# Retention projections of a two-layer hybrid trunk: blocks of 256 weight columns become blocks of 512, with six weight slots and tokens in pairs

## Chip, core and metric

One core of a Trainium2 chip runs the whole kernel. The metric is the device time of one execution in microseconds (us), as the median of three runs. The profile is of one more execution.

## What is computed

Two layers work on a residual stream of 1024 tokens by 1024 features. In each, one projection makes everything that the token mixer needs: queries, keys, values and forget logits of eight attention heads (64 wide), and queries, keys, values and gates of four retention heads (128 wide). The retention part, cut to what matters here:

```
rq, rk, rv, rg = x @ w_in[:, ...]            # (1024 tokens) x (4 heads x 128) each
q = rotary(rq); k = rotary(rk) * 128**-0.5
for each chunk of 128 tokens:
    o = (q k^T * decay) v + (q * xi) state
    state = chunk_decay * state + (k * zeta)^T v
out = silu(rg) * groupnorm(o) * gain
```

After it come the attention heads, one output projection with a layer norm, and a feed-forward part (1024 to 4096 to 1024, squared ReLU) with a second layer norm. All of it is float32; the matrix products are split (below).

## The kernel before

**Products.** Each float32 operand is split into a high part, rounded to the matrix engine's reduced float32 type, and a low part, the rest. `split` (L158, L159) makes them: ScalarE (ACT) casts the high part, VectorE (DVE) subtracts for the low one. `mm3` (L220) then makes three matmuls for each slice of 128 input features: low by high, high by low, high by high. In the retention projections the stationary operand is a tile of 128 tokens (`act`), and the moving operand is the weights (`whi`, `wlo`).

**Weights.** `load_next` takes the next key of one fixed order, starts a DMA on SyncE's queue into one of two staging buffers (`wst`, L205), and splits it into one of four slots (`whi`, `wlo`, a ring of `RING = 4`). `weight(key)` asks for a key and calls `load_next` until the two keys after it (`AHEAD = 2`) are emitted. A key is always 512 KB: here 512 input features by 256 columns, so that a block of 256 columns has two keys.

**The stage.** `retention(l, r, ...)` runs twice in a layer, each time for two of the four heads (256 columns). In each it projects four names one after the other: `rq`, `rk`, `rg`, `rv`. `project(name)` walks over four pairs of token tiles. A pair shares one PSUM bank: two token tiles by 256 columns, 2 x 8 x 3 = 48 matmuls. `bank()` hands out four banks in turn. After a pair, the program first emits what uses the bank, then calls `tick()`, which counts down deferred work, and after every second pair it emits `weight_sums` (L972 to L980): a 1 MB load `wr` from the feed-forward weights, four DVE sums `ts`, and a 1 MB store. These sums are for the feed-forward part.

- `rq` and `rk`: eight DVE instructions rotate a bank (`ra`, `rb`, L393), four GpSimd (POOL) instructions add them up (`nrq`, `nrk`, L398 and L399), and two ticks later four TensorE (PE) transposes (L379) and an ACT copy (L381) follow.
- `rg`: ACT takes the SiLU of a bank (`gt`, L411), POOL multiplies it by the gains (L413).
- `rv`: ACT copies a bank (`rvt`, L463). Two ticks later come the scores and state products (L421, L424), a tick after that the outputs (L441, L443), the group norm, and a store to `r_d` (L455).

After the stage comes the first attention projection (`project_qk`, heads 0 and 1), then attention with the other projections as filling.

**Order.** The program gives the instructions of each engine in this order, but a planner reorders them: the kernel is traced under `tile.TileContext(nc, schedule_with_timeline_sim=True)`, which lays the instructions out by its own estimate of when each could run, the earlier one in the program first among those that are ready. On the chip each engine then goes through its list in that fixed order, and waits on semaphores where an operand or a buffer isn't ready.

**Memory.** Tiles live in pools. Pool `p1v_l` is open for the value projection, `p1r_l` for the stage, `p2_l` for the attention behind it; a later pool takes the memory of an earlier one, and a tile waits for those tiles whose place it takes.

Of the kernel before, what the change touches and what calls it, by code (L numbers as in the profile page):

```python
# [17 lines left out]
P = 128  # L18
# [23 lines left out]
HALF_ROOM = 56  # L42
# [33 lines left out]
def hybrid_trunk(ctx: ExitStack, tc, x, w_in, w_out, w_ff1, w_ff2, ln1_g, ln1_b, ln2_g, ln2_b,  # L76
# [25 lines left out]
    V.memset(half, -0.5)  # L102

# [34 lines left out]
    def defer(n, fn):  # L138
        waiting.append([n, fn])
# [27 lines left out]
    def spec(key, ap):  # L167
        specs[key] = ap
        order.append(key)

    for l in range(L):
# [9 lines left out]
        for r in range(2):  # L181
            for name, c0 in (("rq", C_RQ), ("rk", C_RK), ("rg", C_RG), ("rv", C_RV)):
                block((name, r), c0 + 256 * r, 256)
# [8 lines left out]
    loaded, emitted, odd_home = {}, [0], [None]  # L192

    def load_next(after=None):
        key = order[emitted[0]]
        emitted[0] += 1
        src = specs[key]
        _, kk, cc = src.shape
        odd = key[1] == "vb"
        home, two = (odd_home[0], 1) if odd else (wp, 2)  # L200
        tags = ("vst", f"vhi{key[2]}", f"vlo{key[2]}") if odd else ("wst", "whi", "wlo")
# [123 lines left out]
    def forget_sums(z, pool):  # L325
# [16 lines left out]
        ones = pool.tile([FH, 512], F32, tag="ones", name=nm("ones"), bufs=1)  # L342
        V.memset(ones, 1.0)
# [14 lines left out]
    def retention(l, r, xT, pool, cos, sin, gn, steps):  # L358
        def project(name):
            w = [weight(l, (name, r), g) for g in range(2)]  # L360
            for tp in range(NT // 2):
                ps = bank()
                for j in range(2):
                    mm3(ps[:, 256 * j : 256 * j + 256], lambda a, k: xT.at(a, k, (2 * tp + j) * P, P),
                        lambda b, k: w[k // 4][b][:, k % 4, :], range(8))
                yield tp, ps
                tick()
                steps[0] += 1
                if steps[0] % 2 == 0:
                    weight_sums(l, steps[0] // 2 - 1, ps)  # L370

        def rotate(name, gt, natural):
            trans = []

            def turn(nat):
                tr = ps_tr.tile([P, 2, 2, P], F32, tag="tr", name=nm("tr"))
                for h in range(2):
                    for j in range(2):
                        PE.transpose(tr[:, h, j, :], nat[:, j, h].rearrange("p a d -> p (a d)"), ident)  # L379
                tq = pool.tile([P, 2, 2, P], F32, tag="t" + name, name=nm("t" + name), bufs=4)  # L380
                A.copy(tq, tr)  # L381
                trans.append(tq)

            for tp, ps in project(name):
                p4 = ps.rearrange("p (t h a d) -> p t h a d", t=2, h=2, a=2)
                ra = pool.tile([P, 2, 2, 2, 64], F32, tag="ra", name=nm("ra"), bufs=2)
                rb = pool.tile([P, 2, 2, 2, 64], F32, tag="rb", name=nm("rb"), bufs=2)
                for j in range(2):
                    tt = 2 * tp + j
                    for h in range(2):  # L390
                        sc = gt[:, tt * RH + 2 * r + h : tt * RH + 2 * r + h + 1]
                        for o, tab in ((ra, cos), (rb, sin)):
                            V.scalar_tensor_tensor(o[:, j, h], p4[:, j, h], sc,  # L393
                                                   tab[:, tt, :].unsqueeze(1).broadcast_to([P, 2, 64]),
                                                   op0=ALU.mult, op1=ALU.mult)
                nat = pool.tile([P, 2, 2, 2, 64], F32, tag="n" + name, name=nm("n" + name), bufs=4 if natural is not None else 2)
                for j in range(2):
                    G.tensor_tensor(nat[:, j, :, 0, :], ra[:, j, :, 0, :], rb[:, j, :, 1, :], op=ALU.subtract)  # L398
                    G.tensor_tensor(nat[:, j, :, 1, :], ra[:, j, :, 1, :], rb[:, j, :, 0, :], op=ALU.add)  # L399
                if natural is not None:  # L400
                    natural.append(nat)
                defer(2, lambda nat=nat: turn(nat))
            return trans

        qT = rotate("rq", gq, None)
        kn = []
        kT = rotate("rk", gk, kn)
        gates = []
        for tp, ps in project("rg"):
            gt = pool.tile([P, 2, 256], F32, tag="gt", name=nm("gt"), bufs=4)  # L410
            A.activation(gt.rearrange("p a b -> p (a b)"), ps, AF.Silu)  # L411
            for j in range(2):
                G.tensor_tensor(gt[:, j, :], gt[:, j, :], gn[:, 256 * r : 256 * r + 256], op=ALU.mult)  # L413
            gates.append(gt)
        states = {}

        def scores(tp, j, vt):
            tt = 2 * tp + j
            pa = ps_tr.tile([P, 512], F32, tag="tr", name=nm("tr"))
            for h in range(2):  # L420
                PE.matmul(pa[:, h * P : h * P + P], kT[tp][:, h, j, :], qT[tp][:, h, j, :], start=True, stop=True)  # L421
            if tt < NT - 1:
                for h in range(2):
                    PE.matmul(pa[:, 256 + h * P : 256 + h * P + P], kn[tp][:, j, h].rearrange("p a d -> p (a d)"),  # L424
                              vt[:, j, h, :], start=True, stop=True)
# [10 lines left out]
        def outputs(tp, j, vt, inner):  # L436
            tt = 2 * tp + j
            po = ps_pv.tile([P, 512], F32, tag="pv", name=nm("pv"))
            for h in range(2):
                hs = slice(h * P, h * P + P)  # L440
                PE.matmul(po[:, hs], inner[:, hs], vt[:, j, h, :], start=True, stop=tt == 0)  # L441
                if tt > 0:
                    PE.matmul(po[:, hs], qT[tp][:, h, j, :], states[tt][:, hs], start=False, stop=True)  # L443
# [10 lines left out]
            G.tensor_tensor(on, on, gates[tp][:, j, :], op=ALU.mult)  # L454
            SP.dma_start(r_d[tt * P : tt * P + P, 256 * r : 256 * r + 256], on)  # L455

        def core(tp, vt):
            inner = [scores(tp, j, vt) for j in range(2)]
            defer(1, lambda: [outputs(tp, j, vt, inner[j]) for j in range(2)])

        for tp, ps in project("rv"):
            vt = pool.tile([P, 2, 2, P], F32, tag="rvt", name=nm("rvt"), bufs=3)
            A.copy(vt.rearrange("p a b c -> p (a b c)"), ps)  # L463
            defer(2, lambda tp=tp, vt=vt: core(tp, vt))
# [183 lines left out]
    def layer(l, xT, nxt):  # L648
        src = x if l == 0 else x_d
        with tc.tile_pool(name=f"p1_{l}", bufs=1, reuse_waits="tile") as pool:  # L650
# [521 lines left out]
```

## Time and profile before

| | |
|---|---|
| median of three runs | 2432.82 us (2430.74 to 2435.23) |
| profiled execution, device time | 2434.84 us |
| profiled execution, span from first to last instruction | 2433.1 us |
| PE busy in the span | 2383.8 us, 13424 matmuls |
| DVE, ACT, POOL busy | 1520.0, 1019.9, 376.1 us |
| mean granted clock of PE | 0.997 of full speed |

The profile counts an engine as busy while at least one of its instructions is in flight. Matmuls overlap each other, so the duration of one is longer than the step from the start of one to the start of the next. PEld is the loading of stationary operands, which overlaps PE. A row of a timeline view merges equal neighbours: start, duration of all together, engine (SPq is SyncE's DMA queue), line, operation, out<-in, shape, how many (x), and in brackets the idle time before with what ended it.

### The profile page before, as it was taken

How to read it: one execution, taken by the hardware profiler on the slowest of the kernel's cores; microseconds unless marked ns; L12 is line 12 of the kernel's file. 1: busy time of each engine (PE TensorE's matmuls, PEld its weight loads, DVE VectorE, ACT ScalarE, POOL GpSimd, SP SyncE). 2: the span in 40 equal slices, each digit the busy share in tenths (PEclk: the TensorE clock that was granted, in tenths of full speed). 3: DMA queues.
4: the chain of work that ended last, by engine and by line, in shares of the span. 5: the costliest groups of instructions: out<-in, count | busy, mean ns of one | idle time of the engine just before them, and what ended most of it. 6: DMA issues, size and time to landing. Idle time of an engine off the chain costs nothing. (4 is left out here: it accounts for less than half of the span.)

```text
span 2433.1 us, 35602 instructions
## 1 busy us (share of the span) xinstructions
PE 2383.8 (98%) x13424; PEld 2065.2 (85%) x13424; DVE 1520.0 (62%) x2720; ACT 1019.9 (42%) x1540; POOL 376.1 (15%) x661
## 2 busy tenths in 40 slices
PE   8999999999999999999999999999999999999997
PEld 8999978787888888888899998877888888888886
DVE  4545547855876667565755554578557766576557
ACT  3212236744644453434321222477364545443331
POOL 0324223610000000000213332345000000000003
PEclk9999999999999999999999999999999999999998
DMA  7455685533354458667545566663324544587664
GB/s 231 158 209 202 203 234 157 143 113 121 100 208 164 143 186 307 209 212 226 167 153 191 191 225 223 180 182 109 121 104 147 182 162 166 200 294 217 198 193 145
DMA packets 243309, 442.68 MB, mean 182 GB/s; under 512 B 25520, under 2 KB 127920, under 8 KB 234944
## 3 DMA queue, kind: packets, MB, share of 16 engines
q1 hardware_dynamic: 240832, 432.01, 54.0%
q10 hardware_dynamic: 2304, 8.39, 0.8%
q8 instruction: 106, 1.74, 0.3%
q14 instruction: 67, 0.55, 0.1%
HBM read 301.85 MB, written 138.48 MB: 181 GB/s over the span
## 5 line engine op out<-in xcount | busy, mean ns | idle before, releaser
L159 DVE TENSOR_TENSOR elo<-est,ehi 128x1024 fp32r<-128x1024 f32 x216 | 260.8, 1221 | 181.4 <-ACT ehi L158 181.2
L158 ACT CAST ehi<-est 128x1024 fp32r<-128x1024 f32 x216 | 226.5, 1054 | 344.0 <-PE pv L1063 120.8
L220 PE MATMUL mm<-whi,act 128*128 128x256 f32 (+1 forms) x1248 | 251.0, 295 | 0.8 <-DVE act L159 0.5
L220 PE MATMUL qk<-whi,act 128*128 128x256 f32 (+1 forms) x1248 | 249.8, 294 | 0.8 <-DVE act L159 0.8
L220 PEld LDWEIGHTS mm<-whi,act 128*128 128x128 f32 x1248 | 202.1, 193 | 5.1 <-DVE act L159 0.8
L220 PEld LDWEIGHTS qk<-whi,act 128*128 128x128 f32 x1248 | 200.2, 191 | 4.4 <-DVE act L159 1.0
L273 POOL TENSOR_SCALAR sd<-mv 128x1 f32<-128x1 f32 x15 | 13.9, 927 | 1211.1 <-DVE mv L270 1210.8
L158 ACT CAST whi<-wst 128x1024 fp32r<-128x1024 f32 (+1 forms) x152 | 128.3, 847 | 161.5 <-PE qk L220 46.7
L853 PE MATMUL qk<-xop,whi 128*128 128x512 f32 x608 | 187.2, 389 | 0.0
L220 PE MATMUL mm<-wlo,act 128*128 128x256 f32 (+1 forms) x624 | 183.5, 294 | 0.7 <-DVE wlo L159 0.7
L220 PE MATMUL qk<-wlo,act 128*128 128x256 f32 (+1 forms) x624 | 181.9, 292 | 0.0
L159 DVE TENSOR_TENSOR wlo<-wst,whi 128x1024 fp32r<-128x1024 f32 (+1 forms) x152 | 148.2, 978 | 38.8 <-ACT whi L158 36.4
L220 PE MATMUL mm<-act,whi 128*128 128x512 f32 x512 | 165.5, 397 | 0.0
L853 PE MATMUL pv<-xop,whi 128*128 128x512 f32 x512 | 157.6, 389 | 0.0
L589 PE MATMUL pv<-pt,vp 128*128 128x256 f32 x640 | 130.3, 306 | 8.1 <-POOL pt L571 5.9
L853 PEld LDWEIGHTS qk<-xop,whi 128*128 128x128 f32 x608 | 114.1, 188 | 23.5
L220 PEld LDWEIGHTS mm<-wlo,act 128*128 128x128 f32 x624 | 120.6, 193 | 2.7 <-DVE wlo L159 1.0
L220 PEld LDWEIGHTS qk<-wlo,act 128*128 128x128 f32 x624 | 119.5, 191 | 1.5
L158 ACT CAST pt<-tr 128x512 fp32r<-128x512 f32 (+1 forms) x160 | 85.7, 538 | 82.3 <-PE tr L566 78.6
L853 PE MATMUL mm<-xop,whi 128*128 128x512 f32 x384 | 118.5, 390 | 1.5 <-DVE xop L159 1.5
L159 DVE TENSOR_TENSOR pt<-tr,pt 128x512 fp32r<-128x512 f32 (+1 forms) x160 | 99.8, 630 | 32.0 <-ACT pt L158 31.1
L853 PE MATMUL qk<-xop,wlo 128*128 128x512 f32 x304 | 118.6, 390 | 0.0
(270 smaller groups left out, 5779.4 us busy)
## 6 DMA issues: line engine op xcount, KB each, us to landing
est<-h_d SPq DMA_DIRECT2D x224, 256.0 KB, 3.8
wst<-in_w_ff_dram SPq DMA_DIRECT2D x76, 512.0 KB, 4.2
wr<-in_w_ff_dram SPq DMA_DIRECT2D x32, 1024.0 KB, 6.3
t_d<-ts SPq DMA_DIRECT2D x32, 1024.0 KB, 4.1
h_d<-hs SPq DMA_DIRECT2D x32, 1024.0 KB, 5.2
est<-t_d SPq DMA_DIRECT2D x128, 256.0 KB, 4.0
wst<-in_w_in_dram SPq DMA_DIRECT2D x52, 512.0 KB, 5.4
h_d<-rest SPq DMA_DIRECT2D x32, 768.0 KB, 5.4
```

The lines of the kernel that those rows point to most:

```text
L158: A.copy(hi, src)
L159: V.tensor_tensor(lo, src, hi.bitcast(F32), op=ALU.subtract)
L220: PE.matmul(ps, lhs(a, k), rhs(b, k), start=first and i == 0 and j == 0, stop=last and i == n - 1 and j == 2)
L273: G.tensor_scalar(sd, mv[:, :, 1], EPS, 1.0, op0=ALU.add, op1=ALU.mult)
L589: PE.matmul(ob[:, (qq % 2) * 256 : (qq % 2) * 256 + 256], vp[:, j, :], pt[b][:, 2 * i : 2 * i + 2, :], start=qq % 2 == 0 and jp == 0 and i ...
L853: PE.matmul(ps, ops[p][a][:, k, :], right[p][b][:, k, :], start=first and k == 0 and n == 0, stop=last and k == 3 and n == 2, skip_group_c ...
```

## The change

Queries and keys of two heads are now projected together as one block of 512 columns (`rqk`: 256 of `rq`, 256 of `rk`), gates and values as another (`rgv`). A token tile fills a whole bank, so a block has eight banks of 8 x 3 = 24 matmuls with 512 columns. A weight key is 256 input features by 512 columns, the same 512 KB, but loaded with two DMAs of 256 KB; a block has four keys. To hold four keys and two ahead, two more slots (`nhi`, `nlo`) lie in the stage's own pool, and a counter (`turn`) sends two of each six keys of this stage, and those of the first attention projection, to them.

`project` walks over pairs of token tiles: the first half of the input features (keys 0 and 1) for both tiles, then the second half (keys 2 and 3) for the first tile, whose bank is then used and ticked, then for the second. `tick()` and `weight_sums` come as often as before (32 and 16 in a layer). The rotation keeps eight DVE instructions for a bank of 512; POOL adds it up in two instructions instead of four. SiLU and the copy of values now each take half a bank. Scores and outputs run for one token tile at a time instead of two. The value projection's `vt` moves to pool `p1v`, and a constant of ones for the forget sums becomes one column that is broadcast.

```diff
-HALF_ROOM = 56
+HALF_ROOM = 48
...
         for r in range(2):
-            for name, c0 in (("rq", C_RQ), ("rk", C_RK), ("rg", C_RG), ("rv", C_RV)):
-                block((name, r), c0 + 256 * r, 256)
+            for name, pair in (("rqk", (C_RQ, C_RK)), ("rgv", (C_RG, C_RV))):
+                for c in range(4):
+                    spec((l, name, r, c), *(wi[:, 2 * c : 2 * c + 2, c0 + 256 * r : c0 + 256 * r + 256] for c0 in pair))
...
-        SP.dma_start(st, src)
-        hi = home.tile([P, kk, cc], F32R, tag=tags[1], name=nm(tags[1]))
-        lo = home.tile([P, kk, cc], F32R, tag=tags[2], name=nm(tags[2]))
+        c0 = 0
+        for ap in parts:
+            SP.dma_start(st[:, :, c0 : c0 + ap.shape[2]], ap)
+            c0 += ap.shape[2]
+        bufs = None
+        if key[1] in ("rqk", "rgv") or key[1:] in (("fq", 0), ("fk", 0)):
+            if turn[0] % 6 >= 4:
+                home, tags, bufs = homes["r"], ("wst", "nhi", "nlo"), 2
+            turn[0] = (turn[0] + 1) % 18
+        kw = {} if bufs is None else {"bufs": bufs}
+        hi = home.tile([P, kk, cc], F32R, tag=tags[1], name=nm(tags[1]), **kw)
+        lo = home.tile([P, kk, cc], F32R, tag=tags[2], name=nm(tags[2]), **kw)
...
-        ones = pool.tile([FH, 512], F32, tag="ones", name=nm("ones"), bufs=1)
-        V.memset(ones, 1.0)
+        ones = ones1[0:FH, :].broadcast_to([FH, 512])
...
         def project(name):
-            w = [weight(l, (name, r), g) for g in range(2)]
-            for tp in range(NT // 2):
-                ps = bank()
-                for j in range(2):
-                    mm3(ps[:, 256 * j : 256 * j + 256], lambda a, k: xT.at(a, k, (2 * tp + j) * P, P),
-                        lambda b, k: w[k // 4][b][:, k % 4, :], range(8))
-                yield tp, ps
-                tick()
-                steps[0] += 1
-                if steps[0] % 2 == 0:
-                    weight_sums(l, steps[0] // 2 - 1, ps)
+            w = {}
+
+            def part(ps, tt, half):
+                for c in (2 * half, 2 * half + 1):
+                    if c not in w:
+                        w[c] = weight(l, name, r, c)
+                mm3(ps, lambda a, k: xT.at(a, k, tt * P, P), lambda b, k: w[k // 2][b][:, k % 2, :],
+                    range(4 * half, 4 * half + 4), half == 0, half == 1)
+
+            for u in range(NT // 2):
+                pair = [(2 * u + j, bank()) for j in range(2)]
+                for tt, ps in pair:
+                    part(ps, tt, 0)
+                for tt, ps in pair:
+                    part(ps, tt, 1)
+                    yield tt, ps
+                    tick()
+                    steps[0] += 1
+                    if steps[0] % 2 == 0:
+                        weight_sums(l, steps[0] // 2 - 1, ps)
...
+        for tt, ps in project("rqk"):
...
+            for h in range(4):
+                c = tt * RH + 2 * r + h % 2
+                sc = (gq if h < 2 else gk)[:, c : c + 1]
+                for o, tab in ((ra, cos), (rb, sin)):
+                    V.scalar_tensor_tensor(o[:, h], p4[:, h], sc, tab[:, tt, :].unsqueeze(1).broadcast_to([P, 2, 64]),
+                                           op0=ALU.mult, op1=ALU.mult)
+            nat = pool.tile([P, 4, 2, 64], F32, tag="nat", name=nm("nat"), bufs=NT)
+            G.tensor_tensor(nat[:, :, 0, :], ra[:, :, 0, :], rb[:, :, 1, :], op=ALU.subtract)
+            G.tensor_tensor(nat[:, :, 1, :], ra[:, :, 1, :], rb[:, :, 0, :], op=ALU.add)
+            natural.append(nat)
+            defer(2, lambda nat=nat: turn(nat))
...
+        def core(tt, vt, gt):
+            inner = scores(tt, vt)
+            defer(1, lambda: outputs(tt, vt, gt, inner))
+
+        for tt, ps in project("rgv"):
+            vt = pool.tile([P, 2, P], F32, tag="rvt", name=nm("rvt"), bufs=5)
+            A.copy(vt.rearrange("p b c -> p (b c)"), ps[:, 256:512])
+            gt = pool.tile([P, 256], F32, tag="gt", name=nm("gt"), bufs=5)
+            A.activation(gt, ps[:, 0:256], AF.Silu)
+            G.tensor_tensor(gt, gt, gn[:, 256 * r : 256 * r + 256], op=ALU.mult)
+            defer(2, lambda tt=tt, vt=vt, gt=gt: core(tt, vt, gt))
...
-            with tc.tile_pool(name=f"p1v_{l}", bufs=1, reuse_waits="tile") as odd_home[0]:
-                project_values(l, xT, pool, prepare, z)
+            with tc.tile_pool(name=f"p1v_{l}", bufs=1, reuse_waits="tile") as part:
+                homes["v"] = part
+                project_values(l, xT, part, prepare, z)
             with tc.tile_pool(name=f"p1r_{l}", bufs=1, reuse_waits="tile") as part:
+                homes["r"] = part
                 forget_sums(z, part)
```

## Rows read from the trace of the kernel before

**Rows 1.** The page, parts 1 and 2: busy time; granted clock in 40 slices.

```profile
PE 2383.8 (98%) x13424; PEld 2065.2 (85%) x13424; DVE 1520.0 (62%) x2720; ACT 1019.9 (42%) x1540; POOL 376.1 (15%) x661
...
PEclk9999999999999999999999999999999999999998
```

**Rows 2.** Both stages: us; PE, PEld, DVE, ACT, POOL busy; clock, DMA.

```profile
64.90:278.80 213.90, 213.90 (x1806) 213.72 (x1805) 115.80 (x306) 45.43 (x73) 66.45 (x110) 1.00 0.54 191
1267.60:1481.50 213.90, 213.90 (x1807) 213.72 (x1805) 116.14 (x306) 45.64 (x73) 65.55 (x110) 1.00 0.54 191
```

**Rows 3.** Groups by shape, PE: two of the retention projections, one of the output projection.

```profile
L220 PE MATMUL mm<-whi,act 128*128 128x256 f32 x1152 | 219.0, 287 | 0.8 <-DVE act L159 0.5 <-ACT whi L158 0.3
...
L220 PE MATMUL mm<-whi,mix 128*128 128x512 f32 x96 | 32.7, 392 | 0.0
```

**Rows 4.** Timeline of PE inside a block of `rk`.

```profile
100.13 0.40 PE L220 MATMUL qk<-whi,act 128*128 128x256 f32 x2
100.37 0.28 PE L220 MATMUL qk<-wlo,act 128*128 128x256 f32 x1
100.49 0.40 PE L220 MATMUL qk<-whi,act 128*128 128x256 f32 x2
```

**Rows 5.** Timeline of PE in the output projection: tokens stationary, 512 weight columns moving.

```profile
562.49 0.62 PE L220 MATMUL mm<-whi,mix 128*128 128x512 f32 x2
...
563.17 0.62 PE L220 MATMUL mm<-whi,mix 128*128 128x512 f32 x2
```

**Rows 6.** Timeline of PE in the first attention projection, right behind the stage.

```profile
280.51 0.62 PE L220 MATMUL mm<-act,whi 128*128 128x512 f32 x2
...
281.21 0.61 PE L220 MATMUL mm<-act,whi 128*128 128x512 f32 x2
```

**Rows 7.** Groups of DVE in the first layer's stage: busy, mean ns, idle before.

```profile
L159 DVE TENSOR_TENSOR wlo<-wst,whi 128x1024 fp32r<-128x1024 f32 x16 | 20.4, 1274 | 10.9 <-ACT whi L158 10.6
...
L976 DVE TENSOR_TENSOR ts<-wr 128x512 f32<-128x512 f32 x15 | 10.4, 690 | 48.3 <-DMA wr<-in_w_ff_dram 48.2
```

**Rows 8.** Groups of ACT in the first layer's stage.

```profile
L453 ACT ACTIVATE on<-pv,nb,rs 128x128 f32<-128x128 f32 x20 | 7.5, 457 | 30.0 <-DVE nb L265 30.0
...
L411 ACT ACTIVATE gt<-qk 128x512 f32<-128x512 f32 x4 | 2.4, 598 | 10.0 <-PE qk L220 10.0
```

**Rows 9.** Groups of POOL in the first layer's stage.

```profile
L413 POOL TENSOR_TENSOR gt<-gt,gn 128x256 f32<-128x256 f32 x16 | 12.3, 792 | 30.1 <-ACT gt L411 30.1
```

**Rows 10.** Timeline of ACT where `rg`'s weights take over `rq`'s slots.

```profile
88.43 1.05 ACT L158 CAST whi<-wst 128x1024 fp32r<-128x1024 f32 x1 [3.73 <-PE qk L220]
```

**Rows 11.** Timeline of DVE there: the two splits, first and last of eight rotations.

```profile
89.52 1.22 DVE L159 TENSOR_TENSOR wlo<-wst,whi 128x1024 fp32r<-128x1024 f32 x1 [0.65 <-ACT whi L158]
90.66 0.34 DVE L393 SCALAR_TENSOR_TENSOR ra<-qk,cst,cos 128x128 f32<-128x128 f32 x1
...
92.47 0.34 DVE L393 SCALAR_TENSOR_TENSOR rb<-qk,cst,sin 128x128 f32<-128x128 f32 x1
...
92.79 1.20 DVE L159 TENSOR_TENSOR wlo<-wst,whi 128x1024 fp32r<-128x1024 f32 x1
```

**Rows 12.** Timeline of SyncE's queue before the stage: the first load for `rk`.

```profile
45.12 0.37 SPq L205 DMA_DIRECT2D wst<-in_w_in_dram  x1
```

**Rows 13.** The tile `wst`: from issue of a load to its landing.

```profile
DMA to landing us min/median/max: 3.4/4.3/8.1
```

**Rows 14.** The longest waits of DVE on a DMA: us in total, times, longest.

```profile
DVE ts L976 <- DMA wr<-in_w_ff_dram: 100.6, 26, 7.6
```

**Rows 15.** Waits of PE alone, same columns.

```profile
PE pv L589 <- POOL pt L571: 5.9, 9, 1.2
...
PE mm L220 <- DVE ev L162: 3.6, 2, 2.0
```

**Rows 16.** Timeline of SyncE's queue at the start of attention, first layer.

```profile
303.75 0.91 SPq L505 DMA_DIRECT2D vp<-v_d  x1
...
309.36 1.29 SPq L480 DMA_DIRECT2D k_d<-ev  x2
```

More of the change, by code (lines that the diff above doesn't have):

```diff
@@ L102, in hybrid_trunk @@
     V.memset(half, -0.5)
+    ones1 = cp.tile([P, 1], F32, tag="ones1", name="ones1")
+    V.memset(ones1, 1.0)
     def small(shape, tag, bufs=2):
@@ L165, in hybrid_trunk, with spec @@
     specs, order, ends = {}, [], []
-    def spec(key, ap):
-        specs[key] = ap
+    def spec(key, *parts):
+        specs[key] = parts
         order.append(key)
@@ L191, in hybrid_trunk @@
     place = {k: n for n, k in enumerate(order)}
-    loaded, emitted, odd_home = {}, [0], [None]
+    loaded, emitted, homes, turn = {}, [0], {}, [0]
     def load_next(after=None):
@@ L196, in load_next @@
         emitted[0] += 1
[L197 to L201, printed above, removed]
+        parts = specs[key]
+        kk, cc = parts[0].shape[1], sum(ap.shape[2] for ap in parts)
+        home, tags, two = wp, ("wst", "whi", "wlo"), 2
+        if key[1] == "vb":
+            home, tags, two = homes["v"], ("vst", f"vhi{key[2]}", f"vlo{key[2]}"), 1
         st = home.tile([P, kk, cc], F32, tag=tags[0], name=nm(tags[0]), bufs=two)
@@ L372, in rotate @@
[L372 to L414, printed above, removed]
+            w = {}
[5 more added lines that the diff above has]
+                    range(4 * half, 4 * half + 4), half == 0, half == 1)
@@ new lines, in project, with turn @@
+            for u in range(NT // 2):
[9 more added lines that the diff above has]
+                        weight_sums(l, steps[0] // 2 - 1, ps)
+        def turn(nat):
+            tr = ps_tr.tile([P, 4, P], F32, tag="tr", name=nm("tr"))
+            for h in range(4):
+                PE.transpose(tr[:, h, :], nat[:, h].rearrange("p a d -> p (a d)"), ident)
+            tq = pool.tile([P, 4, P], F32, tag="tqk", name=nm("tqk"), bufs=NT)
+            A.copy(tq, tr)
+            turned.append(tq)
@@ new lines, in retention @@
+        turned, natural = [], []
+        for tt, ps in project("rqk"):
+            p4 = ps.rearrange("p (h a d) -> p h a d", h=4, a=2)
+            ra = pool.tile([P, 4, 2, 64], F32, tag="ra", name=nm("ra"), bufs=2)
+            rb = pool.tile([P, 4, 2, 64], F32, tag="rb", name=nm("rb"), bufs=2)
+            for h in range(4):
+                c = tt * RH + 2 * r + h % 2
[8 more added lines that the diff above has]
+            defer(2, lambda nat=nat: turn(nat))
@@ L434, in scores, with outputs @@
             return inner
-        def outputs(tp, j, vt, inner):
-            tt = 2 * tp + j
+        def outputs(tt, vt, gt, inner):
             po = ps_pv.tile([P, 512], F32, tag="pv", name=nm("pv"))
@@ L440, in outputs @@
                 hs = slice(h * P, h * P + P)
-                PE.matmul(po[:, hs], inner[:, hs], vt[:, j, h, :], start=True, stop=tt == 0)
+                PE.matmul(po[:, hs], inner[:, hs], vt[:, h, :], start=True, stop=tt == 0)
                 if tt > 0:
-                    PE.matmul(po[:, hs], qT[tp][:, h, j, :], states[tt][:, hs], start=False, stop=True)
+                    PE.matmul(po[:, hs], turned[tt][:, h, :], states[tt][:, hs], start=False, stop=True)
             st = small([P, 2, 6], "rst")
@@ L453, in outputs @@
                 A.activation(on[:, hs], po[:, hs], AF.Identity, bias=nb[:, h : h + 1], scale=rs[:, h : h + 1])
-            G.tensor_tensor(on, on, gates[tp][:, j, :], op=ALU.mult)
+            G.tensor_tensor(on, on, gt, op=ALU.mult)
             SP.dma_start(r_d[tt * P : tt * P + P, 256 * r : 256 * r + 256], on)
[L457 to L464, printed above, removed]
+        def core(tt, vt, gt):
[8 more added lines that the diff above has]
+            defer(2, lambda tt=tt, vt=vt, gt=gt: core(tt, vt, gt))
     def project_qk(l, p, xT, pool=None):
```

9 lines of the change are left out of this document (4 added, 5 removed).

## The prediction

> **What bounds the kernel now.** I read the page first. PE is busy for 98% of the span at a granted clock of 1.0 in nearly every slice, which is 2.4 GHz [rows 1], so a change counts by what it does to the list of PE, or by a wait that it gives PE. Then the stage that the change touches, by stretches: it lasts 213.9 us in each layer, and PE is busy in every one of them, while DVE has work for 116 us, ACT for 46 and POOL for 66 [rows 2]. There is no wait of PE to remove here; the stage ends when PE is through its list. So the question is what a matmul costs, and the reader must not take that from the groups. There a 256-column matmul has a mean of 287 ns and a 512-column one of 392 [rows 3], by which two of the first would cost 182 ns more than one of the second, 280 us over the kernel. But these are durations of overlapping instructions. What one takes from its successor is the step between starts, and the timeline shows that: three 256-column matmuls start 0.36 us apart (100.13 to 100.49), 120 ns each [rows 4].
>
> **The sum on PE.** Before, one call of `retention` makes 4 names x 4 pairs x 48 = 768 matmuls of 256 columns, so 3072 in two calls and two layers: 1024 triples x 0.36 = 368.6 us. After, it makes 2 blocks x 8 tiles x 24 = 384 of 512 columns, 1536 in all, 512 triples. The trace has no such matmul in this stage. The nearest one in roles (tokens stationary, 512 weight columns moving) is in the output projection, with 0.68 us for a triple, 227 ns each [rows 5]: 348.2 us, **20.5 us less**. For the bound on the other side I take the slowest triple right behind the stage, 0.70 us [rows 6]: 358.4 us, 10.2 us less. I choose 0.68, since the roles are the same and DVE reads other banks there too.
>
> The rest of PE's list stays: the same transposes, scores and outputs. In one layer they are 213.9 - 512 x 0.36 = 29.6 us, so I expect a stage of 256 x 0.68 + 29.6 = 203.7 us. Gone are 1536 matmuls of the 13424.
>
> The Trainium skill has a rule that speaks against the size of this gain. Its page TensorE: Matmul & The Clock Gate, section Back-to-back issue gap, gives a step of N/2.4 + 2.5 ns for N columns at full clock: 109.2 ns for 256 and 215.8 for 512. By that, a pair saves 2.5 ns, not 13.4, and the change saves an estimated 3.8 us, to 2429.0. The trace has 120 and 227 [rows 4, 5] and does not agree; the sum goes by the rows.
>
> **DVE, ACT and POOL in the shorter stage.** DVE keeps its list (eight rotations for a bank, the splits, the sums `ts`). With its 48.3 us of waiting for the load `wr` [rows 7] it is taken for 116 + 48 = 164 us in a layer, below 203.7. ACT's 16 passes over a bank become 32 over half a bank. A half-bank pass is not in the trace; it lies between 457 ns (128 columns) and 598 ns (512) [rows 8], so 14.6 to 19.1 us instead of 9.6, and ACT comes to 50 to 55 us. POOL's adding goes from 64 instructions to 32 of twice the width, at most 792 ns each, that of the gains [rows 9]: 25 us, inside the 66 that it has. None of the three becomes the bound; I cost them at nothing. The ones that are no longer set cost nothing either: that stood on DVE, in its idle time.
>
> **The weight slots.** A block needs keys 2 and 3 only after 24 matmuls, 5.4 us. Three times in a layer their slots come from the block just before (keys 0 and 1 of `rqk`, of `rgv`, of the second `rqk`), and those are last read 24 matmuls before its end. That gives 10.9 us from the free slot to its use. The trace shows what a handover takes: ACT stands 3.73 us until the slot is free at 88.43 [rows 10], and the second low part is ready at 93.99 [rows 11], with eight rotations in between: 5.6 us. Cover remains for 5.3. ACT and DVE run their lists in order; behind the waiting cast stand copies and SiLUs that empty banks, and those have time, since a bank is wanted again only a pair later (10.9 us). If DVE stands for `wr` just then, at most 7.6 us [rows 14], a handover is 2.3 us late; six such are 14 us. I take nothing and keep 14 as a bound.
>
> The loads go into `wst` and don't wait for the slots, so they can come early. There are 32 more of them on SyncE's queue (two for a key), 0.37 us each [rows 12]: 12 us of issuing in 428 us of the two stages, with nobody behind them who is due.
>
> **The transposes.** For the first tile of a pair the program now puts the transposes 12 matmuls (2.7 us) behind its bank; for the second 36 (8.2 us). Eight rotations take 2.2 us (starts 0.26 us apart, the last 0.34 long) [rows 11], and two additions up to 1.6 [rows 9], 3.8 in all. So the first tile's transposes would be 1.1 us early, and the planner has to move them behind matmuls. If it places them too tightly, PE waits. Such waits exist where PE follows POOL closely, in attention: 9 waits of 0.66 us in the mean, the longest 1.2 [rows 15]. There are 16 such tiles: at most 19 us, 10.5 at the mean. Since the stage has no wait at all now [rows 2], I allow for one wait of the mean, 0.7 us.
>
> **What follows the stage.** The first attention projection's weights now lie in the stage's pool to the end, and the attention pool takes that memory over. A load such as `vp` at 303.75 may have to wait for the last of these matmuls and hold up the queue, the `k_d` stores at 309.36 with it [rows 16]; PE has two waits of 2.0 us at most there, 3.6 in all [rows 15]. These may go (3.6 us less) or double. I take nothing.
>
> **The rivals.**
>
> *A, part of the gain given back:* the handovers or the transposes make PE wait. At the mean wait of rows 15 for every first tile it is 2412.3 + 10.5 = 2423; with all handovers late 2426. For it: both are new and tighter than before. Against: the margins above.
>
> *B, nothing saved:* time goes with the columns, 256 x 0.469 ns, and not with the instructions; two 256-column matmuls are then worth one of 512 columns and the time stays at 2432.8. Against it stands the measured 0.68 for 0.72. The Trainium skill's rule above (TensorE: Matmul & The Clock Gate, Back-to-back issue gap) lies near this case, at 2429.0.
>
> *C, slower, by loads that come late:* the program emits the loads of keys 2 and 3 where keys 0 and 1 are first used. Issued there, they land after a median of 4.3 us, at most 8.1 [rows 13], then the cast takes 1.05 and the low part 1.22 [rows 10, 11]; the cover is 5.4. A block loses 1.2 to 5.0 us, the eight blocks 9 to 39, which gives 2422 to 2452. It is slower than before by more than 0.2% from 3.2 us a block on, a landing of 6.3 us. Against it: `rk`'s first load, which the program emits with the first of `rq` at 64.9, was issued at 45.12, as soon as its staging buffer was free [rows 12].
>
> **How the numbers follow.** The sum against the profiled execution's own 2434.84 us gives 2414.3. The median of the runs is 2.0 lower, so 2412.3 there, and with the one wait **2413.0**. What a measurement of this kernel can tell from no change is about 0.2%, 4.9 us: 2428 to 2437.7. Chances: the forecast, 2407 to 2418, 0.66; A, 2418 to 2428, 0.18 (C at the median landing is in it); B, 0.02; a mixture of A and C that ends within 0.2%, 0.06; C in its dear half, 0.08. So faster 0.84, same 0.08, slower 0.08. The range: below, the waits behind the stage gone (2409) and the runs' own spread of 2; above, all handovers late, 2426. That leaves out 0.19.
>
> **What would show it.** Right: 1536 PE matmuls fewer; triples 0.68 us apart in the stage; the stage near 204 us in both layers with PE busy throughout. Slots: waits of PE on `whi`, `wlo`, `nhi` or `nlo` at the eight block halves would be A or C, and for C the loads would be issued inside the block that needs them. Transposes: waits of PE on the POOL tile `nat`. Wrong altogether: a triple of 0.72 us or more, or PE idle for over 2 us in each block.

## The result, and the profile after

The changed kernel takes 2422.55 us in the median (2418.38 to 2424.49, four runs) against 2432.73 (four runs): a ratio of 0.995 with a 95% interval of 0.9937 to 0.9964. That is 10.2 us less: inside the range of 2407 to 2426, but beyond the 2407 to 2418 that the forecast gave itself, and half of the 20.5 us that the sum had for the steps of PE. The page of the profiled execution, which took 2424.44 us, to be read beside [rows 1]:

```profile
PE 2364.4 (98%) x11888; PEld 1984.5 (82%) x11888; DVE 1520.2 (63%) x2719; ACT 1025.1 (42%) x1572; POOL 359.3 (15%) x597
...
PEclk9999999999999999999999999999999999999999
```

PE has 1536 matmuls fewer, as the sum says. The timeline of PE inside a block of the stage (compare [rows 4, 5]), first behind four transposes, then plain triples:

```profile
83.13 0.60 PE L396 MATMUL tr<-cst,nat 128*128 128x128 f32 x4
83.49 0.48 PE L233 MATMUL mm<-whi,act 128*128 128x512 f32 x1
83.80 0.39 PE L233 MATMUL mm<-wlo,act 128*128 128x512 f32 x1
84.03 0.61 PE L233 MATMUL mm<-whi,act 128*128 128x512 f32 x2
...
140.32 0.39 PE L233 MATMUL mm<-nlo,act 128*128 128x512 f32 x1
140.55 0.61 PE L233 MATMUL mm<-nhi,act 128*128 128x512 f32 x2
141.00 0.39 PE L233 MATMUL mm<-nlo,act 128*128 128x512 f32 x1
```

A triple takes 0.68 us (140.32 to 141.00), the value predicted. The first matmul behind a group of transposes takes 0.31 instead of 0.23 (83.49 to 83.80).

At its end the stage now overlaps with the first attention projection in another way than before, so I measure both together: from the last value matmul to the 96th matmul of that projection. Two layers of the kernel before, then two of the changed one (columns as in [rows 2]):

```profile
64.90:305.55 240.65, 240.65 (x1946) 236.67 (x1945) 128.47 (x349) 52.70 (x89) 76.29 (x130) 1.00 0.56 194
1267.60:1508.20 240.60, 240.60 (x1946) 236.62 (x1945) 128.49 (x349) 52.87 (x89) 75.39 (x130) 1.00 0.56 194
```

```profile
64.50:296.09 231.59, 231.59 (x1178) 195.87 (x1177) 129.01 (x350) 55.98 (x106) 66.80 (x98) 1.00 0.60 203
1266.45:1498.04 231.59, 231.59 (x1178) 195.86 (x1177) 128.61 (x350) 55.72 (x106) 67.71 (x98) 1.00 0.60 202
```

PE is busy in all of it in both kernels, and each layer is 9.0 us shorter, 18.1 in all. So the gain of the stage arrived, and some 8 us of it were lost elsewhere. The next stretch, from there to the last matmul of the output projection (the rest of the projections, attention, output), first before, then after:

```profile
305.55:594.47 288.92, 278.58 (x1594) 231.48 (x1592) 179.62 (x448) 151.32 (x290) 91.91 (x180) 1.00 0.49 150
1508.20:1798.68 290.48, 280.77 (x1593) 232.96 (x1592) 180.03 (x448) 151.32 (x290) 91.86 (x180) 0.99 0.50 150
```

```profile
296.09:592.43 296.34, 280.71 (x1593) 234.28 (x1592) 180.20 (x447) 150.99 (x289) 92.49 (x180) 0.99 0.49 145
1498.04:1788.69 290.65, 278.03 (x1593) 231.45 (x1592) 180.17 (x447) 150.83 (x289) 92.72 (x180) 1.00 0.50 149
```

With the same instructions, in another order, it is 7.6 us longer (586.99 against 579.40), nearly all in the first layer. The difference of the first two numbers of a row is PE's idle time: 10.3 and 9.7 us before, 15.6 and 12.6 after. The waits of PE alone (columns as in [rows 15]) name the place. One line of before that [rows 15] does not have, then three of after:

```profile
PE tr L566 <- DVE pt L159: 1.1, 4, 0.4
```

```profile
PE pv L592 <- POOL pt L574: 12.4, 11, 2.4
PE tr L569 <- DVE pt L162: 7.2, 11, 1.2
...
PE mm L233 <- DVE ev L162: 2.0, 2, 1.4
```

The waits for `ev` of [rows 15] are down from 3.6 to 2.0, and the stage has none at all, neither on weights nor on `nat`. But the values' matmuls of attention now wait for POOL at `pt` (the transposed attention scores: ACT and DVE split them, POOL zeroes a corner) for 12.4 us instead of 5.9, and the transposes for DVE at `pt` for 7.2 instead of 1.1. The longest of the waits for POOL, on POOL's timeline, on PE's, and in stretches of 5 us (columns as in [rows 2]):

```profile
410.75 0.95 POOL L556 TENSOR_SCALAR sc<-sc,ri 128x384 f32<-128x384 f32 x1 [0.33 <-DVE ri L555]
416.56 0.20 POOL L515 TENSOR_SCALAR ref<-ncb 128x4 f32<-128x4 f32 x1 [4.86 <-DMA ncb<-c_d]
416.85 1.15 POOL L522 TENSOR_SCALAR rel<-ncb,ref 128x256 f32<-128x256 f32 x2
417.97 0.69 POOL L556 TENSOR_SCALAR sc<-sc,ri 128x512 f32<-128x512 f32 x1
418.61 0.21 POOL L574 MEMSET pt<- 128x128 f32 x1
```

```profile
418.87 0.38 PE L592 MATMUL pv<-pt,vp 128*128 128x256 f32 x1 [2.44 <-POOL pt L574]
420.81 0.38 PE L592 MATMUL pv<-pt,vp 128*128 128x256 f32 x1 [1.56 <-POOL pt L574]
```

```profile
418.00:423.00 5.00, 2.58 (x12) 2.10 (x13) 0.76 (x2) 0.24 (x1) 3.78 (x8) 0.85 0.06 20
423.00:428.00 5.00, 5.00 (x35) 4.46 (x34) 3.50 (x11) 4.90 (x13) 3.82 (x7) 0.81 0.97 301
```

POOL runs its list in order. It stands 4.86 us for the load of `ncb`, and the zeroing of a 128x128 corner of `pt`, which needs nothing of that load, stands behind it with `rel` and `sc`. PE waits 2.44 and 1.56 us, and right behind these waits the granted clock falls: 0.85 and 0.81 in two stretches of 5 us are 1.5 and 1.9 us at 0.5, the level of 1.2 GHz.

It is one of two such drops in this layer. The other begins at 322.5, also with 3.4 us at 0.5, and there PE had stood for the scaling `sc` and for `ev`:

```profile
320.88 0.55 PE L569 MATMUL tr<-cst,sc 128*128 128x128 f32 x3 [0.93 <-POOL sc L556]
322.79 0.80 PE L233 MATMUL mm<-act,wlo 128*128 128x512 f32 x1 [1.36 <-DVE ev L162]
```

The kernel before has a drop of that second kind too, at 1521.9 in its second layer, behind a wait of 1.99 us for `ev`.

### The profile page after: what moved, and what is told of

It reads as the page before. It is cut to its first block, busy times and chain, and to the rows that moved or that the text cites. A ratio compares the mean times of both kernels' runs of the same rounds, so it can differ in the third digit from the quotient of the medians.

```text
span 2422.6 us, 32508 instructions
## 1 busy us (share of the span) xinstructions
PE 2364.4 (98%) x11888; PEld 1984.5 (82%) x11888; DVE 1520.2 (63%) x2719; ACT 1025.1 (42%) x1572; POOL 359.3 (15%) x597
## 5 line engine op out<-in xcount | busy, mean ns | idle before, releaser
L233 PE MATMUL mm<-whi,act 128*128 128x512 f32 (+1 forms) x608 | 187.2, 373 | 1.0 <-DVE act L162 0.5
L233 PE MATMUL qk<-whi,act 128*128 128x512 f32 (+1 forms) x608 | 186.4, 373 | 0.8 <-DVE act L162 0.8
L161 ACT CAST whi<-wst 128x512 fp32r<-128x512 f32 (+1 forms) x140 | 115.8, 829 | 168.4 <-PE qk L233 36.0
L162 DVE TENSOR_TENSOR wlo<-wst,whi 128x512 fp32r<-128x512 f32 (+1 forms) x140 | 133.1, 954 | 40.4 <-ACT whi L161 39.7
L592 PE MATMUL pv<-pt,vp 128*128 128x256 f32 x640 | 133.4, 310 | 13.1 <-POOL pt L574 12.4
L233 PEld LDWEIGHTS mm<-whi,act 128*128 128x128 f32 x608 | 111.8, 191 | 19.8 <-ACT whi L161 0.9
L233 PEld LDWEIGHTS qk<-whi,act 128*128 128x128 f32 x608 | 110.3, 189 | 18.6 <-DVE act L162 1.0
L553 ACT ACTIVATE sc<-sc,mx 128x128 f32<-128x128 f32 (+7 forms) x128 | 99.4, 777 | 43.5 <-DVE mx L547 40.3
L233 PE MATMUL mm<-wlo,act 128*128 128x512 f32 (+1 forms) x304 | 113.2, 373 | 0.7 <-DVE wlo L162 0.7
L858 PEld LDWEIGHTS pv<-xop,whi 128*128 128x128 f32 x512 | 96.1, 188 | 19.9
L233 PE MATMUL qk<-wlo,act 128*128 128x512 f32 (+1 forms) x304 | 112.2, 369 | 0.0
```

The source lines that it names most:

```text
L161: A.copy(hi, src)
L162: V.tensor_tensor(lo, src, hi.bitcast(F32), op=ALU.subtract)
L233: PE.matmul(ps, lhs(a, k), rhs(b, k), start=first and i == 0 and j == 0, stop=last and i == n - 1 and j == 2)
L553: A.activation(sc[:, 0:ne], sc[:, 0:ne], AF.Exp, bias=mx, scale=-1.0, accum_out=sm)
L592: PE.matmul(ob[:, (qq % 2) * 256 : (qq % 2) * 256 + 256], vp[:, j, :], pt[b][:, 2 * i : 2 * i + 2, :], start=qq % 2 == 0 and jp == 0 and i ...
L858: PE.matmul(ps, ops[p][a][:, k, :], right[p][b][:, k, :], start=first and k == 0 and n == 0, stop=last and k == 3 and n == 2, skip_group_c ...
```

## The experiments

**The theories.** The theory of the steps says that the stage's gain is real and that the rest of the change costs some 7 us in attention. Its rivals are that the stage gains less than it seems, or that the loss is an accident of one execution or one order. For the loss itself there were then theories of its cause: landings that vary; the order in which the planner happened to put attention; the new slots in the stage's pool, with that order; the pairs of tokens; the load of `ncb`; and POOL's zeroing. The profiles are compared by three numbers of the two layers: the stage with the projection; the rest, up to the end of the output projection; and PE's idle time in the rest. The table stands at the end of this section.

**The change once more.** The kernel as changed, timed with others on one chip.

> The changed kernel, unchanged. In its first profile the stage's matmuls step 17 us less in the two layers together, and 7 us of that are gone at the end of the first layer's attention, near nothing in the second's, though PE's order there is the same in both layers. Theory 1 (the loss is waits on DMA landings that vary): median 2418 to 2425, and the loss of the two attentions is shared out differently. Rival (the loss lies in the order): the first layer's attention loses its 7 us again.

Measured: 2424.4 us against 2434.35, ratio 0.9958 (0.9945 to 0.9971). The stage is 231.9 and 231.6, and the loss lies in the rest again, but it is now 4.3 and 3.1 us in the two layers where it was 7.4 and 0.2. Every engine has the same list, so how the waits fall differs between executions; that some 7.5 us are lost is the same in these two.

**Blocks of 512 columns as two halves.** All of the change is kept, but `part` computes a bank with two sets of 256-column matmuls (the last argument only lets them share the bank).

```diff
-                mm3(ps, lambda a, k: xT.at(a, k, tt * P, P), lambda b, k: w[k // 2][b][:, k % 2, :],
-                    range(4 * half, 4 * half + 4), half == 0, half == 1)
+                for c0 in (0, 256):
+                    mm3(ps[:, c0 : c0 + 256], lambda a, k: xT.at(a, k, tt * P, P),
+                        lambda b, k: w[k // 2][b][:, k % 2, c0 : c0 + 256],
+                        range(4 * half, 4 * half + 4), half == 0 and c0 == 0, half == 1 and c0 == 256, True)
```

> Every 512-column matmul of the stage is cut into two of 256 columns; blocks, slots, pairs and pools stay. Step theory: the steps go back to 0.36 us for a triple, so some 17 to 20 us come back, 2440 to 2443, slower than the kernel before by 7 to 10, since what attention loses stays. Rival (attention loses because PE reaches it earlier): at the old pace it loses nothing, 2432 to 2434. Second rival (pairs, slots and pools win or lose time by themselves in the stage): the stage differs from 213.9 us by over 2.

Measured: 2441.21 us against 2434.35, ratio 1.0021 (1.0012 to 1.003), so 16.8 us more than the changed kernel in the same comparison; its stage is back at 240.5 and 241.3 us. The steps are worth what the trace says, and the rest of the change costs 6.9 us.

**Another order, for both kernels.** `FILL`, a list of numbers that says how many steps of the other projections go between the steps of attention, is changed in the same way in both kernels. It was meant to move the attention's matmuls, and did so only in the second pair. With 26 and 10 every engine of either kernel has the list of its original, by the names and shapes in the traces: this pair is a repetition. With 14 and 22, some 60 of the 1593 matmuls of each layer's rest stand elsewhere, all behind the waits shown above (from 457 us on in the first layer).

```diff
-FILL = (18, 18, 18, 18, 18, 18, 4, 4)
+FILL = (26, 10, 26, 10, 26, 10, 4, 4)
...
-FILL = (18, 18, 18, 18, 18, 18, 4, 4)
+FILL = (14, 22, 14, 22, 14, 22, 4, 4)
```

> The changed kernel with other numbers in FILL (26 and 10 steps of the projections in turn, in place of 18 and 18), which moves only the filling inside attention and with it the planner's order there. With its twin below it forms a pair at one FILL. Theory 2 (what attention gives back, 7 to 8 us, is the chance of one order, and the gain of the change itself is the 17 us of its steps): the difference of the pair is not 10 but anywhere between 5 and 20, and its mean over the pairs lies near 17. Rival (pairs, slots and pools cost attention a fixed 7 us): every pair differs by 9 to 11.

> The kernel before with the same numbers in FILL (26 and 10), the other half of the pair. Theory 2: it moves against 2434 by some us in either direction, and not by as much as its twin. Rival: both move by the same amount.

> The changed kernel with 14 and 22 steps in turn in FILL. A second pair for the same question: by theory 2 the waits of PE for the tile pt and the clock's drops behind them come and go with the order, 2412 to 2426; by the rival it stays 9 to 11 us below its twin.

> The kernel before with 14 and 22 steps in turn in FILL, the other half of the second pair. Theory 2: 2428 to 2440 and another difference than in the first pair. Rival: 9 to 11 us above its twin.

Measured: 2425.44 (0.9957, 0.9942 to 0.9972) against 2434.17 (0.9994, 0.9984 to 1.0004), and 2424.32 (0.9957, 0.9942 to 0.9972) against 2435.12 (1.0001, 0.9992 to 1.001). The pairs differ by 8.7 and 10.8 us, as the original pair does (10.2), so the loss comes again in each comparison. Whether it hangs on the order they can't say, since they hardly moved it; the next experiment can.

**The slots alone.** The kernel before, with two more slots in the stage's pool, used for the first attention projection's first keys; `vt` and the ones moved as in the change.

```diff
+        if key[1:] in (("fq", 0), ("fk", 0)):
+            home, tags, kw = stage_home[0], ("wst", "nhi", "nlo"), {"bufs": 2}
-        hi = home.tile([P, kk, cc], F32R, tag=tags[1], name=nm(tags[1]))
+        hi = home.tile([P, kk, cc], F32R, tag=tags[1], name=nm(tags[1]), **kw)
```

> The kernel before with the memory parts of the change alone: two more slots in the stage's pool for the weights of the first attention projection, the value projection's vt in its own pool, the broadcast ones; blocks stay 256 wide, one name after the other. Theory 3 (these slots change when the first attention projection's weights and the attention's tiles are ready in the plan, and so the order in attention): the waits of transposes for DVE pt (1.1 us before, 7.2 in the changed kernel) and of PE for POOL pt (5.9, 12.4) appear here too, and the time is 2439 to 2443. Rival (the attention's loss comes from the stage's new blocks and their tail): waits as before and 2432 to 2436.

Measured: 2434.86 us against 2434.14, ratio 1.0006 (0.9997 to 1.0015). Its attention has the order of the changed kernel, matmul for matmul, and nearly its waits in number, but those for POOL at `pt` are shorter:

```profile
PE pv L594 <- POOL pt L576: 9.1, 10, 1.6
PE tr L571 <- DVE pt L162: 7.7, 12, 1.2
```

PE's idle time is 11.3 and 11.7 us, there is no drop of the clock in attention, and the time is that of before. These parts of the change bring the order; the order alone costs nothing.

**The first attention projection back in the ring of four.**

```diff
-        if key[1] in ("rqk", "rgv") or key[1:] in (("fq", 0), ("fk", 0)):
+        if key[1] in ("rqk", "rgv"):
...
-            turn[0] = (turn[0] + 1) % 18
+            turn[0] = (turn[0] + 1) % 16
```

> The weights of the first attention projection go back to the ring of four slots, so that the attention pool no longer waits for them; the rest is the changed kernel. If the loss in attention came from that memory being taken over late, the start of attention has no more PE waits on the evacuation tile ev (2.0 us) and the time falls to 2414 to 2418. If not, 2420 to 2425, with the order at the start of attention slightly moved.

Measured: 2432.53 us, ratio 0.9993 (0.9984 to 1.0002), slower than either of the two ranges. The takeover of the memory, feared in the prediction, is not the loss: without it the kernel is 8 us slower than the changed one in the same comparison, and PE stands twice for its bank at the start of attention, as the waits show (the longest, 4.7 us, at 310.25).

```profile
PE pv L592 <- POOL pt L574: 11.6, 14, 1.6
PE mm L233 <- DVE ev L165: 9.3, 2, 4.7
```

**The stage's keys in the ring of four.** The two extra slots serve the first attention projection alone.

```diff
-        if key[1] in ("rqk", "rgv") or key[1:] in (("fq", 0), ("fk", 0)):
-            if turn[0] % 6 >= 4:
-                home, tags, bufs = homes["r"], ("wst", "nhi", "nlo"), 2
-            turn[0] = (turn[0] + 1) % 18
+        if key[1:] in (("fq", 0), ("fk", 0)):
+            home, tags, bufs = homes["r"], ("wst", "nhi", "nlo"), 2
```

> The changed kernel with the stage's keys in the ring of four alone; the two more slots only take the first attention projection's two keys. With pairs, keys 0 and 1 of the next block get their slots 24 matmuls (5.4 us) before its start and take 3.7 us. My theory: just enough, PE waits under 1 us a block, 2422 to 2428. Rival (the six slots carry the gain): waits on the weights of 2 us and more at each of six block starts, 2434 and more.

Measured: 2422.75 us, ratio 0.9954 (0.9935 to 0.9973): the same as the changed kernel, with no wait in the stage. The stage does not need six slots.

**Tokens one at a time.** In `project` both halves of a tile's features run before the next tile.

```diff
                 for tt, ps in pair:
                     part(ps, tt, 0)
-                for tt, ps in pair:
                     part(ps, tt, 1)
```

> The changed kernel with token tiles one at a time: all four keys are wanted within 24 matmuls of a block's start, and the first keys' slots come free 2.7 us before a block's end, not 5.4. The handover took 3.7 us in the changed kernel's trace (104.3 to 108.0), with 9.3 us left until key 2 was wanted. My theory: 3.7 is still below the 5.4 of cover, PE does not wait for weights, and the time is 2422 to 2427. Rival (pairs carry the gain): PE waits at the handovers, up to 2 us each at six places, 2430 and more.

Measured: 2428.4 us, ratio 0.9981 (0.9972 to 0.999), outside what I expected. The stage has one wait of 0.55 us in the first layer, of a transpose for POOL's `nat`, and none in the second. PE does not wait for weights, so the pairs aren't what covers the handover either. The 6 us against the ring of four (same comparison) are lost in attention again (idle time 14.2 and 16.2).

**`ncb` on a DMA queue of its own.**

```diff
-            SP.dma_start(ncb, rows(c_d[h], P))
+            A.dma_start(ncb, rows(c_d[h], P))
```

> The loads ncb of attention go out on ACT's DMA queue instead of SyncE's, where they stand behind the loads of keys and queries; the rest is the changed kernel. Theory: POOL stands for ncb, and the zeroing of pt and the scaling of sc, for which PE waits, stand behind it on POOL; with ncb landing earlier the waits of PE for POOL pt (12.4 us) fall below 6 and the time to 2414 to 2418. Rival: the waits have another cause, and the time stays at 2420 to 2425.

Measured: 2427.32 us, ratio 0.9966 (0.9954 to 0.9978): no gain. The waits for POOL at `pt` are 11.3 us, 13 of them. But the edit also changed the order of attention, and the waits for `ev` grew from 2.0 to 7.4 us. At the place shown above less is lost: neither layer has a drop of the clock there, and in the 25 us from the issue of that load PE is idle for 1.8 and 1.5 us, where the changed kernel's profile has 5.7 and 4.5. So this run doesn't clear the load of blame; it shows that the edit as a whole does not pay.

**The zeroing off POOL.** The zeroing of `pt` goes to DVE; nothing else changes.

```diff
-                        G.memset(pt[a][:, 0, :].bitcast(F32), 0.0)
+                        V.memset(pt[a][:, 0, :].bitcast(F32), 0.0)
```

> The changed kernel with one edit: the 128 zeroings of the tile `pt` in attention go from POOL (205 ns each) to DVE. In the profile of the changed kernel the values' matmuls wait 12.4 us in all (11 waits, up to 2.4 us) for POOL at that tile, the largest single entry among the waits of PE in attention; the kernel before has 5.9 us there (9 waits). If these waits of PE, and the drops of the granted clock right behind the longest of them, are what attention gives back, they go with the edit: 6 to 8 us less, about 2414 to 2417 us (ratio 0.992 to 0.9935), and the kernel beats both. If they are only the place where the lateness of something else shows (loads, DVE, ACT), the same idle time comes back under other names (DVE's or ACT's half of `pt`, the scaling `sc`, the banks), and the time stays at 2420 to 2426 us (ratio 0.995 to 0.997). The planner sets the order of attention anew, which by the earlier pairs is worth about 2 us either way.

Measured: 2411.71 us (2408.56 to 2421.61, six runs) against 2434.54, ratio 0.991 (0.9893 to 0.9927). It beats both kernels, by more than the first range had. The waits of PE:

```profile
PE tr L569 <- POOL sc L556: 8.3, 6, 1.5
...
PE tr L569 <- DVE ri L555: 2.7, 4, 0.9
PE tr L569 <- DVE pt L574: 2.6, 6, 0.8
...
PE tr L569 <- DVE pt L162: 1.4, 6, 0.3
```

Those of 12.4 us are gone. Part of them comes back at the scaling `sc`, which still stands behind `ncb` on POOL (1.5 us became 8.3), and 2.6 at the zeroing on DVE. The rest of the two layers, for which PE was idle 15.6 and 12.6 us, now has 11.0 and 10.2:

```profile
296.93:587.00 290.07, 279.11 (x1593) 0.99 0.51 148
1493.47:1783.86 290.39, 280.15 (x1593) 0.99 0.50 149
```

The profiled execution is the longest of the six, 2421.61. It shows 6.5 us less in the rest (580.46 against 586.99) and 3.7 us more outside it, 2.0 of them in the last layer's feed-forward; the runs that were not profiled reach 2409. The gain in the median is 10.8 us (from two comparisons), so these rows explain only a part of it. The planner's order of attention is also another one again: some 490 of the 1593 matmuls of a layer's rest stand elsewhere. What the zeroing's new place and what the new order is worth is not told apart.

A zeroing takes 165 ns on DVE and 205 on POOL in the groups by form. The Trainium skill (Trainium Architecture — The Big Picture, The five engines, in one table) has POOL two times slower than DVE at streaming elementwise work; 205 against 165 does not agree for this one. The difference of 0.04 us is small beside waits of up to 2.4 us, so I take it that the list that it stood in mattered, and not its duration.

The numbers of the profiled executions, layer by layer. The last column is the time at a granted clock of 0.5 in the rest:

| kernel | stage and projection, us | rest, us | PE idle in it, us | at 0.5, us |
|---|---|---|---|---|
| before | 240.6, 240.6 | 288.9, 290.5 | 10.3, 9.7 | 0, 3.4 |
| before, `FILL` 26 | 240.6, 240.6 | 290.2, 289.5 | 11.2, 10.6 | 0, 0 |
| before, `FILL` 14 | 241.6, 240.6 | 289.6, 289.7 | 10.2, 8.6 | 0, 3.4 |
| slots alone | 240.6, 240.6 | 288.5, 289.8 | 11.3, 11.7 | 0, 0 |
| changed | 231.6, 231.6 | 296.3, 290.7 | 15.6, 12.6 | 6.8, 0 |
| changed once more | 231.9, 231.6 | 293.2, 293.6 | 12.8, 13.6 | 6.8, 3.4 |
| changed, `FILL` 26 | 231.6, 231.6 | 296.0, 295.4 | 13.8, 13.5 | 10.2, 6.8 |
| changed, `FILL` 14 | 231.6, 231.6 | 295.4, 291.0 | 13.0, 12.1 | 10.2, 0 |
| two halves | 240.5, 241.3 | 296.7, 290.4 | 14.3, 11.2 | 10.2, 3.4 |
| back in the ring | 231.6, 231.6 | 298.8, 295.9 | 14.8, 14.5 | 10.2, 3.4 |
| ring of four | 231.6, 231.6 | 292.9, 293.1 | 14.4, 13.5 | 0, 3.4 |
| no pairs | 232.6, 231.6 | 295.2, 298.2 | 14.2, 16.2 | 6.8, 6.8 |
| `ncb` on its own queue | 231.6, 231.6 | 293.3, 292.1 | 14.2, 11.6 | 0, 3.4 |
| zeroing on DVE | 231.6, 231.6 | 290.1, 290.4 | 11.0, 10.2 | 3.4, 6.8 |

A least-squares fit over the 26 layers of the executions profiled before the last experiment gives rest = 279.2 + 0.96 x idle + 0.41 x time at 0.5, with 0.7 us left over (root mean square, 1.6 at most). Idle time counts about in full, as it must, since the rest of a layer is PE's busy and idle time together. What the fit adds is the price of the clock: a drop of 3.4 us makes a layer some 1.4 us longer, one of 6.8 us some 2.8.

## Why the prediction was half right

*The sum on PE.* Right in its mechanism, and somewhat too large. It had 1024 triples of 0.36 us become 512 of 0.68, 20.5 us less; the steps of the retention matmuls add up to 373.3 us before and 356.1 after, 17.2 less. Single triples are 0.36 and 0.68 as taken, but the means are 0.365 and 0.695. Of the 3.9 us that a layer has over 256 x 0.68 after the change, 2.9 are 33 steps of 0.31 to 0.32 behind other work, 20 of them behind transposes like that at 83.49. The kernel before has 30 such steps of 0.20, 2.5 us over, so these hardly touch the difference. Most of the 3.2 us by which the sum was too large lies in the plain steps: their mean is 228 ns after the change, and not the 226.7 that a triple of 0.68 gives. The stage with the projection gained 18.1, 9.0 to 9.1 in a layer, where the forecast had 10.2 (213.9 to 203.7).

The Trainium skill's rule of N/2.4 + 2.5 ns (TensorE: Matmul & The Clock Gate, Back-to-back issue gap) would have had the blocks save 3.8 us. The two-halves experiment has 16.8, so the measurement does not agree with it and the row that was taken instead does. The prediction left out that the same section gives this rule for a single, isolated matmul, and for a stream of weight loads and matmuls, as here, a measured 131 ns at 512 columns; the 227 ns of this case agree with neither figure. What the 13 ns by which a pair of 256 columns costs more than one of 512 consist of, no run shows.

*DVE, ACT and POOL in the stage at nothing.* Right: PE is busy in all 231.59 us. ACT has 3.3 us more than before (55.98 against 52.70).

*The slots and loads.* Right, with more room than predicted. Where the key slots of a block come free, in the timelines of ACT, DVE and PE:

```profile
104.31 1.05 ACT L161 CAST whi<-wst 128x1024 fp32r<-128x1024 f32 x1 [6.26 <-PE qk L233]
```

```profile
105.39 2.58 DVE L162 TENSOR_TENSOR wlo<-wst,whi 128x1024 fp32r<-128x1024 f32 x2 [2.88 <-ACT whi L161]
```

```profile
117.35 0.39 PE L233 MATMUL mm<-whi,act 128*128 128x512 f32 x1
```

ACT gets the slot at 104.31, the second low part is ready at 107.97, and the block that needs them begins key 2 at 117.35. The handover takes 3.7 us where 5.6 was estimated. Rival C did not come: no wait on a weight. Two experiments add that neither the six slots nor the pairs are needed for it.

*The transposes.* One wait of 0.7 us was allowed; there is none.

*What follows the stage: the step that failed.* "I take nothing", with bounds of 3.6 us on both sides. It measured 7.6 us. I had looked there for loads behind the taken-over memory, and at the two waits for `ev`; those waits got shorter, as one bound had it (though one of them has a drop of the clock behind it), and the kernel that does without the takeover is 8 us slower. What I passed over stood in [rows 15] itself: PE follows POOL closely in attention, and I used that row as a price for the transposes of the stage and not as a risk where it was measured. So rival A, with a chance of 0.18 for 2418 to 2428, had the size of what was given back, but not the place. That the time still lies in the range is luck: its upper end, 2426, stood for handovers that come late, and none did.

*What is shown of the cause, and what is open.* The changed kernel loses its time in attention, by longer waits of PE (idle 28.2 us in the two layers' rests against 20.0) and by drops of the clock behind them. The order of attention alone is not the cause: in slots alone, two halves and the changed kernel every engine has the same list of instructions in the rest, by names and shapes, and so has SyncE's queue of loads and stores, and slots alone loses nothing. So I take it that the difference lies in when things arrive. The traces show it for one load, that of `ncb` at the place above. In the changed profile POOL uses it 10.9 and 9.1 us after its issue, in slots alone 8.0 and 8.7, in the kernel before 8.8 and 7.4. In the 26 layers of the table without its last row, all nine in which this takes 9.6 us or more have a drop of the clock at that place; of the 17 in which it takes 9.1 or less, two have one. That ties the load, POOL's list, PE's wait and the clock together at this place, though it is a match in the traces and not an experiment.

Why the load lands later in the changed kernel is not settled. Two halves (10.4 and 8.9 us) and slots alone have the same stage to within 0.8 us, and still differ by 6.4 us in time (2441.21 against 2434.86, from two comparisons). What differs between them is how the stage fetches and hands over weights, so that other transfers may reach attention at another time; that is only argued. Open too is how much of the 10.8 us is owed to the zeroing's place and how much to the new order that came with it, and what the zeroing on DVE would bring to the kernel before, which has 5.9 us of the same waits: that was not run.

## What to carry to other kernels

Price a matmul by the steps between starts in a timeline; by the means of the groups the change would have been worth 280 us. When a stage that PE fills without a gap gets shorter, look at the next stage's closest waits as well and price them there. And look at what stands in front of a small instruction on an engine that runs in order: 128 zeroings of 0.2 us stood behind work that waits for a load, and the kernel with them elsewhere is 10.8 us faster, as much as the change itself had gained (10.2), though its new order may have a part in that.

## What the runs showed of the hardware

Two short waits of PE, 2.44 and 1.56 us with one matmul between, were followed by 3.4 us at a granted clock of 0.5 (1.2 GHz). The fit puts such a drop at 1.4 us. Waits of 0.67 and 1.56 us at the same place of the second layer had none behind them.

The first 512-column matmul behind four transposes of 128 columns took 0.31 us to the next start instead of 0.23. In the kernel before the same place costs as much (202 ns instead of 120), so it did not change the difference.

Two executions of one program shared out the same loss differently over two equal layers: 7.4 and 0.2 us, then 4.3 and 3.1.
